# Sliding-window logits of the last 128 queries as two fp32r passes, and an order table with a third level

## The chip, the core and the metric

One core of a Trainium2 chip runs the kernel. The metric is device time in microseconds (us); the median of three runs is compared. Engines: PE is TensorE, DVE is VectorE, ACT is ScalarE, POOL is GpSimd, SP is SyncE, which issues the loads.

## The reference, cut to what matters

The model is a trunk of two layers over 256 tokens of width 1024 in fp32. The even layer has a gated linear attention (GLA, 4 heads) beside a sliding-window attention (SWA: 8 query heads on 2 key/value heads of width 64, window 128), then an output projection; the odd layer has 8 MoBA heads of width 128 and an output projection. The change touches the logits of SWA:

```python
qb = q.reshape(B_, NB, W, KVH, G, DH).transpose(0, 3, 4, 1, 2, 5)   # blocks of W = 128 queries
kb, vb = band(k), band(v)                                          # previous and own block: 256 keys
...
logits = jnp.einsum('bkgnqd,bknsd->bkgnqs', qb, kb).astype(jnp.float32) * (DH ** -0.5) + bias
logits = jnp.where(mask, logits, -jnp.inf)
...
probs = jax.nn.softmax(jnp.concatenate([logits, sink], axis=-1), axis=-1)[..., :-1]
o = jnp.einsum('bkgnqs,bknsd->bkgnqd', probs.astype(v.dtype), vb)
```

So the last 128 queries need, for each of 8 heads, a 128 x 256 product over 64 channels.

## The kernel before, in words

**Precision.** Most fp32 products are made of three fp32r products: an operand is split into a high part (its value rounded to fp32r) and a low part (the rest). `wh` and `wl` are the parts of a block of weights, `xh` and `xl` those of the activations, `pTh` and `pTl` those of the attention probabilities, `ogh` and `ogl` those of the gated outputs. A high part is a copy (`nc.copy`, on ACT or on DVE), a low part a subtraction (DVE). Projections write the PSUM tiles `pj`, logits the tiles `s`, transposes `t`, sums of attention `o`. The logits of SWA are plain fp32 matmuls in before, with `qT` and `kb` as they are; a tile `qT` has four heads in its 128 partitions, in two columns of blocks: for each pair of heads, key head 0 sits in partitions 0 to 63 and key head 1 in partitions 64 to 127.

**Order.** The code is recorded first, as nodes; `Plan.order` then simulates the engines and picks for each engine the ready node with the highest rank. A rank is the longest path of costs from the node to the end, plus a boost, plus numbers of the table `BOOST` for the node's stage (`nc.label`: "start", "bk", "bq", "swa1", ...) and for the stage with its engine ("swa1.PE"). `nc.together(pieces, cost)` joins several matmuls into one node; the first is then issued at line 179 and the others at line 160. Everything else is issued at line 179 too, so the names of tiles tell the work, save for a copy in its form for DVE, which has line 82. Tiles come from rings (4 `raw` buffers for loaded weights, 6 of `wh` and `wl`, 4 PSUM `pj`), and loads stand in the one queue of SP in order.

**SWA.** `swa(t)` makes the logits of query block t: for t = 0, 8 matmuls of 128 keys in one joined node; for t = 1, two joined nodes of 4 matmuls with 256 keys each, in the order head pair by head pair, with key heads 0 and 1 in turn, each on 64 rows of the array:

```python
for i, kv in nc.together([(i, kv) for i in its for kv in range(2)], 1450 if t else 1850):
    b = slice(64 * kv, 64 * kv + 64)
    nc.tensor.matmul(pvs[kv][:, i - i0, :], qb[i // 2][b, i % 2, t * P:(t + 1) * P], kb[b, 0:n],
                     start=True, stop=True)
```

Projections of other stages stand around these nodes on PE, as the table decides.

Of the kernel before, what the change touches and what calls it, by code (L numbers as in the profile page):

```python
# [11 lines left out]
F32 = mybir.dt.float32  # L12
F32R = mybir.dt.float32r
# [6 lines left out]
P = 128  # L20
D = 1024
S = 256
# [27 lines left out]
class Plan:  # L50
# [165 lines left out]
    def order(self):  # L216
        nodes = self.nodes
        for n in reversed(nodes):
            own = n.cost + n.tail + (2000 + n.dma / 400.0 if n.dma else 0)
            n.path = max((u.path + (n.cost + 2 if u.eng == n.eng == "PE" else own + self.latency(n, u))  # L220
                          for u in n.users if not u.load), default=own)
        for n in nodes:
            n.rank = 1e6 - n.idx if n.load else (
                n.path + n.boost + (BOOST.get(n.label, 0.0) + BOOST.get(n.label + "." + n.eng, 0.0)))
        clock = dict.fromkeys(self.ENGINES, 800.0)
        cand = {e: [] for e in self.ENGINES}
        table, dma = None, 0.0
        bank = {}

        def ready(n, e):  # L230
            return max([n.ready] + [t + self.latency(n, n) for b in n.banks for o, t in bank.get(b, {}).items() if o != e])

        for n in nodes:
            n.left, n.ready = len(n.deps), 0.0
            if not n.left:
                for e in n.forms:
                    cand[e].append(n)
        result, queue = [], [n.idx for n in nodes if n.eng == "SP"]
        while len(result) < len(nodes):
            best = None  # L240
            for e, c in cand.items():
                if e == "SP":
                    c = [n for n in c if n.idx == queue[0]] if queue else []
                if not c:
                    continue
                when = {n.idx: ready(n, e) for n in c}
                first = max(clock[e], min(when.values()))

                def gain(n):
                    return n.rank - (PENALTY if n.table and n.table != table else 0)  # L250

                pick = max((n for n in c if when[n.idx] <= first), key=gain)

                soon = [n for n in c if first < when[n.idx] <= first + LOOK and n.rank > gain(pick) + MARGIN]
                if soon and e != "SP":
                    pick = max(soon, key=lambda n: n.rank)
                    first = when[pick.idx]
                if best is None or (first, first + pick.forms[e][0]) < (best[0], best[0] + best[1].forms[best[2]][0]):
                    best = (first, pick, e)
            start, n, n.eng = best  # L260
            for e in n.forms:
                cand[e].remove(n)
            if n.eng == "SP":
                queue.pop(0)
            cost, tail, _ = n.forms[n.eng]
            if n.eng == "PE" and start < COLD:
                cost *= 1.85
            if n.table and n.table != table:
                table, cost = n.table, cost + 1283
            end = start + cost  # L270
            n.start = start
            clock[n.eng] = end
            if n.dma:
                dma = max(dma, start + (1500 if n.eng != "POOL" else 2500)) + n.dma / 400.0
                tail = dma + 500 + LATE - end
            result.append(n)
            for u in n.users:
                u.left -= 1
                u.ready = max(u.ready, end + 2 if u.eng == n.eng == "PE" else end + tail + self.latency(n, u))
                if not u.left:  # L280
                    for e in u.forms:
                        cand[e].append(u)
            n.end = end + tail
            for b in n.banks:
                bank.setdefault(b, {})[n.eng] = max(n.end, bank.get(b, {}).get(n.eng, 0.0))
        self.span = max(n.end for n in nodes)
        return result
# [6 lines left out]
SIZE = {F32: 4, F32R: 4, BF16: 2, I8: 1}  # L294


BOOST = {"start": 573258, "start.DVE": -38538, "start.POOL": 52750, "start.ACT": 1243, "start.PE": 40662, "rstd": 209951, "rstd.ACT": 127208, "rstd.DVE": 113369, "rstd.POOL": -103238, "rstd.PE": -63184, "bk": 369539, "bk.PE": 13356, "bk.DVE": 198, "bq": 14881, "bq.PE": -11180, "bq.DVE": -1220256, "decay": -52551, "decay.PE": 66981, "decay.ACT": 61712, "decay.DVE": 9116, "bg": 10969, "bg.ACT": -64523, "bg.PE": -41970, "swa0": -4537, "swa0.PE": -352320, "swa0.POOL": -37746, "swa0.DVE": -9500, "swa0.ACT": -51324, "aq": -112180, "aq.ACT": -85453, "aq.DVE": -223051, "aq.PE": 79963, "ak": -100825, "ak.ACT": 151115, "ak.PE": -242853, "swa1": 68756, "swa1.PE": 23420, "swa1.POOL": 181142, "swa1.DVE": -59955, "swa1.ACT": -94554, "gla": 18982, "gla.PE": 34789, "gla.ACT": -128852, "gla.DVE": -7061, "gla.POOL": 19304, "ag": -184974, "ag.ACT": -42703, "ag.DVE": -62205, "ag.PE": -215469, "agate": -1314, "agate.ACT": -116486, "agate.DVE": 11971, "agate.PE": 43490, "oe": -524223, "oe.ACT": -21502, "oe.DVE": -34920, "oe.PE": 17533, "h1": 4121, "h1.DVE": -77200, "h1.PE": -15335, "h1.ACT": 8186, "h1.POOL": 164832, "odd": -21419, "odd.PE": 30523, "odd.DVE": 68575, "cv": 3851, "cv.ACT": -41808, "cv.DVE": -1217, "cv.PE": 230720, "ck": -791503, "ck.ACT": 48816, "ck.DVE": 120, "ck.PE": 58567, "q0": 60721, "q0.ACT": -448094, "q0.DVE": 15032, "q0.PE": -52983, "g0": -464, "g0.ACT": 35308, "g0.DVE": 7665, "g0.PE": 13119, "moba0": -18143, "moba0.PE": 26122, "moba0.DVE": -25038, "moba0.ACT": 99267, "q1": 12325, "q1.ACT": -288835, "q1.DVE": -22989, "q1.PE": -4150, "g1": 4635, "g1.ACT": -23792, "g1.DVE": -131311, "g1.PE": 3161, "moba1": -8670, "moba1.PE": 15882, "moba1.DVE": 124820, "moba1.ACT": -179903, "oo": -68254, "oo.ACT": 638, "oo.DVE": -312970, "oo.PE": -5575, "tail": 23837, "tail.DVE": 29969, "tail.ACT": -40694, "tail.POOL": -8207, "tail.SP": -33334}
COLD = 6500
WARM = 7
PENALTY, LATE, LOOK, MARGIN = 12000, 600, 130, 1500  # L300
# [3 lines left out]
def trunk(ctx: ExitStack, tc: tile.TileContext, t_in, out):  # L304
    real, nc = tc.nc, Plan(tc.nc)
# [343 lines left out]
    def swa(t):  # L649
        n = P * (t + 1)  # L650
        probs = [[], []]
        for i0 in range(0, 4, 4 // (t + 1)):

            pts = [ps("s") for kv in range(2)]
            pvs = [pt.rearrange("p (h c) -> p h c", c=n) for pt in pts]
            its = range(i0, i0 + 4 // (t + 1))
            for i, kv in nc.together([(i, kv) for i in its for kv in range(2)], 1450 if t else 1850):
                b = slice(64 * kv, 64 * kv + 64)
                nc.tensor.matmul(pvs[kv][:, i - i0, :], qb[i // 2][b, i % 2, t * P:(t + 1) * P], kb[b, 0:n],
                                 start=True, stop=True)  # L660
            for kv in range(2):
                probs[kv] += softmax(t, [4 * kv + i for i in its], pvs[kv], 0, nsink)
        og = buf("og", [P, 4, P], F32, 2)
        low = buf("low", [P, 4, P])
        for kv in range(2):
            po = weigh(t, probs[kv], [(bvs[:, :, kv], 0), (bvs[:, :, kv], 1)])
            own, other = slice(64 * kv, 64 * kv + 64), slice(64 - 64 * kv, 128 - 64 * kv)
            nc.copy(low[own], po[other])
            nc.vector.tensor_add(og[own], po[own], low[own])
        gated(og, og, sgb, t, slice(0, P))  # L670
        to_operand(0, t, 4, og)
# [4 lines left out]
    kb = buf("kb", [P, S])  # L676
    nc.vector.tensor_mul(kb, o[:, 0], rr[0])


    nc.label = "bq"  # L680
    def bias_of(h, t, far):
# [5 lines left out]
                       ap=[list(a.ap[0]), [-first * step if t else P, n], [-1, P]])  # L687

    o = project_cols("bq", xh[0], xl[0], 1)
    qb = []  # L690
    for i in range(2):
        q = buf("qT", [P, 2, S], F32, 3)
        nc.vector.tensor_mul(q, o[i], rr[1].unsqueeze(1).to_broadcast([P, 2, S]))
        qb.append(q)

    nc.label = "decay"

# [69 lines left out]
    for t in range(NT):  # L767
        c0 = t * P
        pv = [ps("s")[:, 0:S].rearrange("p (h c) -> p h c", h=2) for e in range(2)]
        for j, e, half in nc.together([(j, e, i) for j in range(2) for e in range(2) for i in range(2)], 750):  # L770
            b = slice(64 * e, 64 * e + 64)
            if half == 0:
                nc.tensor.matmul(pv[e][0:64, j, :], ke[b, j, c0:c0 + 64], qx[b, j, c0:c0 + P], start=True, stop=True)
# [6 lines left out]


    pS = ps("o")
    for h in nc.together(range(4), 740):
        b = slice(64 * (h % 2), 64 * (h % 2) + 64)
        nc.tensor.matmul(pS[b, h * P:(h + 1) * P], kdt[:, h * 64:(h + 1) * 64], va[0][:, h * P:(h + 1) * P],
                         start=True, stop=True)
# [229 lines left out]
```

## Time and profile before

| | before |
|---|---|
| median of 3 runs | 213.86 us (213.02 to 214.02) |
| profiled execution, its own time | 213.65 us |
| its span in the trace | 211.9 us |
| granted TensorE clock, mean | 0.994 |
| PE busy | 202.8 us (96%), 1431 matmul records |
| PEld busy (weight loads) | 182.5 us (86%) |
| DVE busy | 175.6 us (83%) |
| ACT busy | 106.3 us (50%) |
| POOL busy | 13.5 us (6%) |
| chain that ended last | PE 82%, DVE 6%, DMA 5%, issue 4% |

Busy time is the union of the records of an engine. Matmuls are pipelined and a record lasts longer than the distance to the next one, so a gap of PE shows best in the distance from one start to the next. The last matmul starts at 205.28 us; what follows it up to 211.9 us is the tail. An fp32 matmul leaves two records, an fp32r matmul one.

### The profile page before, as it was taken

Reading aid. Unit: us, or ns where it says so; the run is one execution under the profiler, and the core shown is the slowest. Engines: PE = TensorE matmul, PEld = TensorE weight load, DVE = VectorE, ACT = ScalarE, POOL = GpSimd, SP = SyncE. Lnnn points to the kernel's source line nnn. Section 1 sums busy time; section 2 is a strip of 40 time slices with the busy share of each in tenths; the row PEclk is TensorE's granted clock in tenths of the full one; section 3 lists DMA queues with packets and bytes.
Section 4 is the critical chain, followed back from the end, with each engine's and each line's share of the span. In section 5 each row is a group of like instructions: output and inputs, shape, how many; then the busy total and the mean of one; then the engine's idle time right before and its main releaser. Section 6 shows DMA issues by size and latency. Waiting matters only on the chain.

```text
span 211.9 us, 3783 instructions
## 1 busy us (share of the span) xinstructions
PE 202.8 (96%) x1431; PEld 182.5 (86%) x1431; DVE 175.6 (83%) x365; ACT 106.3 (50%) x206; POOL 13.5 (6%) x38
## 2 busy tenths in 40 slices
PE   7899999999999999999999999999999999999970
PEld 2899999999977777887789999998999999788870
DVE  3997888998999999996985866996889998966551
ACT  3568544793789538462263700404386465910221
POOL 5007000000110000310001010000000000000101
PEclk9999999999999999999999999999999999999997
DMA  6998988786620003497045481087751443120012
GB/s 210 408 410 333 356 302 263 260 281 189 199 98 3 2 0 99 120 328 248 17 186 197 153 298 49 5 295 295 261 172 69 162 138 99 17 82 3 26 73 99
DMA packets 10913, 36.05 MB, mean 170 GB/s; under 512 B 1344, under 2 KB 1808, under 8 KB 10896
## 3 DMA queue, kind: packets, MB, share of 16 engines
q1 hardware_dynamic: 10464, 35.13, 47.7%
q10 hardware_dynamic: 432, 0.69, 0.9%
q8 instruction: 11, 0.18, 0.4%
q14 instruction: 6, 0.05, 0.1%
HBM read 34.76 MB, written 1.05 MB: 169 GB/s over the span
## 4 chain that ended last, share of the span: by engine, by line
PE 82%; DVE 6%; DMA 5%; issue 4%; SPq 1%; ACT 1%; POOLq 0%; POOL 0%; ACTq 0%; DVEq 0%
PE pj L179 63%; PE s L179 8%; PE o L179 7%; PE t L179 3%; DMA raw<-in_q 3%; DMA raw<-in_xav 2%; DVE neg L179 1%; PE s L160 1%; DVE wl L179 1%; DVE pTl L179 1%; DVE wh L82 1%; DVE pTh L82 1%; SPq L179 1%; ACT wh L179 1%; DVE junk L179 0%
## 5 line engine op out<-in xcount | busy, mean ns | idle before, releaser
L179 DVE TENSOR_TENSOR wl<-raw,wh 128x1024 fp32r<-128x1024 f32 (+2 forms) x59 | 68.1, 1169 | 6.5 <-ACT wh L179 3.4
L179 PE MATMUL pj<-xh,wh 128*128 128x256 f32 x224 | 56.1, 288 | 0.2 <-ACT wh L179 0.2
L179 PE MATMUL pj<-xh,wl 128*128 128x256 f32 x224 | 55.8, 287 | 0.0
L179 PE MATMUL pj<-xl,wh 128*128 128x256 f32 x224 | 55.5, 288 | 0.0
L179 ACT ACTIVATE wh<-raw 128x1024 fp32r<-128x1024 f32 (+2 forms) x37 | 37.4, 1017 | 32.9 <-DMA raw<-in_q 11.1
L179 PEld LDWEIGHTS pj<-xh,wh 128*128 128x128 f32 x224 | 39.2, 191 | 0.9 <-ACT wh L179 0.6
L179 PEld LDWEIGHTS pj<-xl,wh 128*128 128x128 f32 x224 | 39.3, 191 | 0.7 <-issue 0.3
L179 PEld LDWEIGHTS pj<-xh,wl 128*128 128x128 f32 x224 | 39.5, 191 | 0.4 <-DVE wl L179 0.2
L82 DVE CAST wh<-raw 128x1024 fp32r<-128x1024 f32 (+2 forms) x22 | 14.6, 666 | 12.4 <-PE pj L179 4.7
L179 PE MATMUL pj<-wl,ogh 128*128 128x512 f32 (+1 forms) x64 | 22.9, 373 | 0.0
L179 PE MATMUL pj<-wh,ogh 128*128 128x512 f32 (+1 forms) x64 | 22.6, 372 | 0.0
L179 PE MATMUL pj<-wh,ogl 128*128 128x512 f32 (+1 forms) x64 | 22.5, 371 | 0.0
L179 PE MATMUL pj<-wh,xl 128*128 128x328 f32 (+2 forms) x64 | 17.4, 336 | 0.6 <-DVE xl L179 0.6
L179 PE MATMUL pj<-wh,xh 128*128 128x328 f32 (+2 forms) x64 | 17.1, 332 | 0.2 <-DVE xh L82 0.2
L179 PE MATMUL pj<-wl,xh 128*128 128x328 f32 (+2 forms) x64 | 17.2, 332 | 0.0
L179 ACT ACTIVATE prob<-neg,mn 128x129 f32<-128x129 f32 (+3 forms) x32 | 14.2, 445 | 3.7 <-DVE mn L179 3.7
L179 PEld LDWEIGHTS pj<-wl,ogh 128*128 128x128 f32 x64 | 12.1, 189 | 2.2 <-DVE wl L179 0.6
L179 PEld LDWEIGHTS pj<-wh,ogl 128*128 128x128 f32 x64 | 12.0, 188 | 1.9 <-DVE ogl L179 0.3
L179 PEld LDWEIGHTS pj<-wh,xh 128*128 128x128 f32 x64 | 11.2, 188 | 2.5 <-DVE xh L82 1.1
L179 PEld LDWEIGHTS pj<-wh,ogh 128*128 128x128 f32 x64 | 11.9, 188 | 1.6 <-ACT ogh L179 0.2
L179 PEld LDWEIGHTS pj<-wh,xl 128*128 128x128 f32 x64 | 11.0, 188 | 1.5 <-DVE xl L179 1.1
L179 ACT ACT_TABLE_LOAD x8 | 10.3, 1283 | 3.8 <-DVE xt L179 1.3
(190 smaller groups left out, 332.5 us busy)
## 6 DMA issues: line engine op xcount, KB each, us to landing
raw<-in_oe SPq DMA_DIRECT2D x8, 512.0 KB, 4.0
raw<-in_q SPq DMA_DIRECT2D x8, 512.0 KB, 4.2
raw<-in_g SPq DMA_DIRECT2D x8, 512.0 KB, 4.4
raw<-in_oo SPq DMA_DIRECT2D x8, 512.0 KB, 3.4
raw<-in_bq SPq DMA_DIRECT2D x4, 512.0 KB, 6.5
raw<-in_bg SPq DMA_DIRECT2D x4, 512.0 KB, 6.0
raw<-in_ag SPq DMA_DIRECT2D x4, 512.0 KB, 4.9
raw<-in_xav SPq DMA_DIRECT2D x4, 456.0 KB, 5.2
```

The costliest lines, as they stand in the source:

```text
L82: lambda: getattr(self.vector._real, name)(*args, **kw))
L160: node.forms = {eng: (node.cost, node.tail, lambda: (emit(), getattr(real, method)(*args, **kw)))}
L179: node.forms = {eng: (node.cost, node.tail, lambda: getattr(real, method)(*args, **kw))}
```

## The change

First, the logits of `swa(1)` become fp32r. A new tile `kbs` has for each key head the high part of the keys twice (in both halves of the partitions) and the low part once (in its own half). A new tile `qs{i}{kv}` has the high part of the queries in its own half and the low part in the other half. Per head there are then two matmuls into the same PSUM region: one over all 128 rows (query high and low, stacked, on key high, twice), and one over 64 rows (query high on key low). They are not joined into one node. Making the tiles takes 8 copies and 6 subtractions of 64 x 256. Second, a rank may also take a number from the table for a stage, an engine and the name of the written tile. The table is new in whole (481 entries against 106). Third, the planner's cost of four joined nodes is lower.

```diff
             n.rank = 1e6 - n.idx if n.load else (
-                n.path + n.boost + (BOOST.get(n.label, 0.0) + BOOST.get(n.label + "." + n.eng, 0.0)))
+                n.path + n.boost + (BOOST.get(n.label, 0.0) + BOOST.get(n.label + "." + n.eng, 0.0)
+                                    + BOOST.get(n.label + "." + n.eng + "." + n.tag[1].split("_")[0], 0.0)))
...
-            for i, kv in nc.together([(i, kv) for i in its for kv in range(2)], 1450 if t else 1850):
-                b = slice(64 * kv, 64 * kv + 64)
-                nc.tensor.matmul(pvs[kv][:, i - i0, :], qb[i // 2][b, i % 2, t * P:(t + 1) * P], kb[b, 0:n],
-                                 start=True, stop=True)
+            if t:
+                for kv in range(2):
+                    b = slice(64 * kv, 64 * kv + 64)
+                    for i in its:
+                        q = qbs[kv, i // 2][:, i % 2]
+                        nc.tensor.matmul(pvs[kv][:, i - i0, :], q, kbs[:, kv, 0], start=True, stop=False)
+                        nc.tensor.matmul(pvs[kv][:, i - i0, :], q[b], kbs[b, kv, 1], start=False, stop=True)
+            else:
+                for i, kv in nc.together([(i, kv) for i in its for kv in range(2)], 1190):
+                    b = slice(64 * kv, 64 * kv + 64)
+                    nc.tensor.matmul(pvs[kv][:, i - i0, :], qb[i // 2][b, i % 2, 0:P], kb[b, 0:n], start=True, stop=True)
...
+    kbs = buf("kbs", [P, 2, 2, S], F32R)
+    for kv in range(2):
+        own, other = slice(64 * kv, 64 * kv + 64), slice(64 - 64 * kv, 128 - 64 * kv)
+        nc.copy(kbs[own, kv, 0], kb[own])
+        nc.copy(kbs[other, kv, 0], kb[own])
+        nc.vector.tensor_sub(kbs[own, kv, 1], kb[own], kbs[own, kv, 0].bitcast(F32))
...
+        for kv in range(2):
+            v = qbs[kv, i] = buf(f"qs{i}{kv}", [P, 2, P], F32R, 1, 512)
+            own, other = slice(64 * kv, 64 * kv + 64), slice(64 - 64 * kv, 128 - 64 * kv)
+            nc.copy(v[own], q[own, :, P:])
+            nc.vector.tensor_sub(v[other], q[own, :, P:], v[own].bitcast(F32))
...
-BOOST = {"start": 573258, "start.DVE": -38538, "start.POOL": 52750, ... }
+BOOST = {"start": 429806, "start.DVE": 47795, "start.DVE.warm0": -30025, ... }
```

In before, PE has the first joined node of the logits of the last 128 queries (`s` from `kb` and `qT`) in one block among the matmuls of a projection (`pj` from `xh`, `xl`, `wh`, `wl`); each row here is one fp32 matmul, and what follows is the first transposes of the probabilities (`t`):

```order
L179 MATMUL pj_73<-xh_71,wh_85 128x256
L179 MATMUL s_122<-kb_123,qT_125 128x256
L160 MATMUL s_124<-kb_123,qT_125 128x256
L160 MATMUL s_122<-kb_123,qT_125 128x256
L160 MATMUL s_124<-kb_123,qT_125 128x256
L179 MATMUL pj_73<-xl_72,wh_85 128x256
```

In the changed kernel the same place on PE has the four fp32r matmuls of key head 0 (128 rows, 64 rows, 128 rows, 64 rows, in this order), a stretch of the projection, and the four of key head 1:

```order
L179 MATMUL pj_73<-xh_71,wh_85 128x256
L179 MATMUL s_122<-kbs_124,qs_127 128x256 x4
L179 MATMUL pj_73<-xl_72,wh_85 128x256
...
L179 MATMUL pj_73<-xl_72,wh_85 128x256
L179 MATMUL s_125<-kbs_124,qs_128 128x256 x4
L179 MATMUL pj_73<-xh_71,wl_86 128x256
```

Further on, the second four heads: key head 0's second pair has one matmul on 128 rows, one on 64, then the four of key head 1 come between, and the last two (128 rows, then 64) stand on both sides of a product of probabilities and values (`o` from `pTh` and `bv`):

```order
L179 MATMUL pj_74<-wl_89,xh_71 128x512
L179 MATMUL s_122<-kbs_124,qs_130 128x256 x2
L179 MATMUL s_125<-kbs_124,qs_131 128x256 x4
L179 MATMUL s_122<-kbs_124,qs_130 128x256
L179 MATMUL o_70<-pTh_158,bv_116 128x512
L179 MATMUL s_122<-kbs_124,qs_130 128x256
L179 MATMUL pj_74<-wh_88,xh_71 128x512
```

What moved: 4 fp32 matmuls twice (16 records in all) became 16 fp32r matmuls, and the 64-row ones stand singly between 128-row ones.

At the program's start PE has in before the four `pj` tiles (`pj_73` and `pj_74` belong to the first 128 tokens, `pj_75` and `pj_76` to the last 128) in turn for each part of the first block of weights (`wh_79`, `wl_80`), and then the second block (`wh_82`):

```order
L179 MATMUL pj_73<-wh_79,xh_71 128x328
L179 MATMUL pj_75<-wh_79,xh_71 128x328
L179 MATMUL pj_74<-wh_79,xh_71 128x328
L179 MATMUL pj_76<-wh_79,xh_71 128x328
L179 MATMUL pj_73<-wh_79,xl_72 128x328
L179 MATMUL pj_75<-wh_79,xl_72 128x328
```

In the changed kernel:

```order
L179 MATMUL pj_73<-wh_79,xh_71 128x328
L179 MATMUL pj_75<-wh_79,xh_71 128x328
L179 MATMUL pj_74<-wh_79,xh_71 128x328
L179 MATMUL pj_73<-wh_79,xl_72 128x328
L179 MATMUL pj_74<-wh_79,xl_72 128x328
L179 MATMUL pj_73<-wl_80,xh_71 128x328
L179 MATMUL pj_74<-wl_80,xh_71 128x328
L179 MATMUL pj_74<-wh_82,xh_71 128x328
L179 MATMUL pj_73<-wh_82,xh_71 128x328
L179 MATMUL pj_74<-wh_82,xl_72 128x328
L179 MATMUL pj_73<-wh_82,xl_72 128x328
L179 MATMUL pj_76<-wh_79,xh_71 128x328
```

Two of the four tiles now run ahead into the second block of weights, and matmuls of the first block for the other two come later. DVE and ACT also share the splitting of the second block in another way: the copy `wh_82` moved from DVE to ACT, and its `xh` from ACT to DVE.

## Rows read from the trace of the kernel before

**Rows 1.** Windows: busy us and count of each engine, granted clock, DMA share, GB/s.

```profile
8.08:205.30 197.22, 196.49 (x1408) 179.15 (x1408) 169.33 (x350) 102.37 (x200) 9.82 (x22) 1.00 0.49 169
20.00:52.30 32.30, 32.30 (x271) 32.26 (x270) 28.96 (x49) 19.89 (x31) 0.86 (x2) 1.00 0.83 278
...
55.00:75.00 20.00, 19.55 (x116) 15.56 (x115) 19.52 (x68) 16.30 (x47) 1.48 (x8) 1.00 0.23 79
```

**Rows 2.** Timeline of PE at the start: start, duration, work, [idle before].

```profile
6.72 0.77 PE L179 MATMUL pj<-wh,xh 128*128 128x328 f32 x4
8.08 0.86 PE L179 MATMUL pj<-wh,xl 128*128 128x328 f32 x4 [0.59 <-DVE xl L179]
```

**Rows 3.** Timeline of PE, two waits: one in SWA, one in the odd layer.

```profile
67.43 0.41 PE L179 MATMUL t<-ident,prob 128*128 128x128 f32 x2 [0.15 <-DVE pTl L179]
...
146.63 0.51 PE L179 MATMUL pj<-xh,wh 128*128 128x256 f32 x2 [0.17 <-ACT wh L179]
```

**Rows 4.** Timeline of PE, the two logits nodes of the last 128 queries.

```profile
58.15 0.28 PE L179 MATMUL pj<-xh,wh 128*128 128x256 f32 x1
58.35 0.70 PE L179 MATMUL s<-kb,qT 64*128 64x256 f32 x2
...
59.91 0.39 PE L179 MATMUL pj<-xl,wh 128*128 128x256 f32 x1
60.13 0.28 PE L179 MATMUL pj<-xh,wl 128*128 128x256 f32 x1
...
62.00 0.40 PE L179 MATMUL pj<-wh,xl 128*128 128x512 f32 x1
62.33 0.48 PE L179 MATMUL s<-kb,qT 64*128 64x256 f32 x1
...
63.90 0.63 PE L179 MATMUL t<-ident,prob 128*128 128x128 f32 x4 [0.29 <-ACT prob L179]
```

**Rows 5.** Timeline of PE, the logits node of the first 128 queries.

```profile
52.42 0.28 PE L179 MATMUL pj<-xh,wl 128*128 128x256 f32 x1
52.55 0.28 PE L179 MATMUL pj<-xh,wh 128*128 128x256 f32 x1
52.76 0.37 PE L179 MATMUL s<-kb,qT 64*128 64x128 f32 x1
...
52.97 0.27 PE L179 MATMUL s<-kb,qT 64*128 64x128 f32 x1
52.98 0.94 PE L160 MATMUL s<-kb,qT 64*128 64x128 f32 x13
53.85 0.39 PE L179 MATMUL pj<-xl,wh 128*128 128x256 f32 x1
54.07 0.28 PE L179 MATMUL pj<-xh,wl 128*128 128x256 f32 x1
```

**Rows 6.** Timeline of PE, an fp32 matmul on 128 rows (odd layer).

```profile
149.06 0.28 PE L179 MATMUL pj<-xh,wl 128*128 128x256 f32 x1
149.18 0.38 PE L179 MATMUL s<-s,qT 128*128 128x128 f32 x2
...
149.52 0.28 PE L179 MATMUL pj<-xh,wl 128*128 128x256 f32 x1
```

**Rows 7.** Timeline of PE, logits in fp32r on 128 rows (odd layer).

```profile
171.87 0.28 PE L179 MATMUL s<-kbs,qs 128*128 128x256 f32 x1
171.99 0.40 PE L179 MATMUL o<-pTh,cv 128*128 128x512 f32 x1
```

**Rows 8.** Groups of instructions on DVE that write small tiles: count, duration ns min/median/max, starts.

```profile
L82 DVE CAST cv<-o x2: 404/408/413, 24.8 to 25.2; 16x256 fp32r<-16x256 f32 x2
...
L179 DVE TENSOR_TENSOR cv<-o,cv x1: 416/416/416, 28.4 to 28.4; 16x256 fp32r<-16x256 f32 x1
```

**Rows 9.** Timeline of DVE at the start.

```profile
7.54 0.88 DVE L179 SCALAR_TENSOR_TENSOR xl<-raw,xt,xh 128x256 fp32r<-128x256 f32 x2
```

**Rows 10.** Timeline of ACT at the start.

```profile
7.11 0.75 ACT L179 ACTIVATE wh<-raw 128x656 fp32r<-128x656 f32 x1 [0.55 <-DMA raw<-in_xav]
```

More of the change, by code (lines that the diff above doesn't have):

```diff
@@ L294 @@
 SIZE = {F32: 4, F32R: 4, BF16: 2, I8: 1}
-BOOST = {"start": 573258, "start.DVE": -38538, "start.POOL": 52750, "start.ACT": 1243, "start.PE": 40662, "rstd": 209951, "rstd.ACT": 127208, "rstd.DVE": 113369, "rstd.POOL": -103238, "rstd.PE": -63184, "bk": 369539, "bk.PE": 13356, "bk.DVE": 198, "bq": 14881, "bq.PE": -11180, "bq.DVE": -1220256, "decay": -52551, "decay.PE": 66981, "decay.ACT": 61712, "decay.DVE": 9116, "bg": 10969, "bg.ACT": -64523, "bg.PE": -41970, "swa0": -4537, "swa0.PE": -352320, "swa0.POOL": -37746, "swa0.DVE": -9500, "swa0.ACT": -51324, "aq": -112180, "aq.ACT": -85453, "aq.DVE": -223051, "aq.PE": 79963, "ak": -100825, "ak.ACT": 151115, "ak.PE": -242853, "swa1": 68756, "swa1.PE": 23420, "swa1.POOL": 181142, "swa1.DVE": -59955, "swa1.ACT": -94554, "gla": 18982, "gla.PE": 34789, "gla.ACT": -128852, "gla.DVE": -7061, "gla.POOL": 19304, "ag": -184974, "ag.ACT": -42703, "ag.DVE": -62205, "ag.PE": -215469, "agate": -1314, "agate.ACT": -116486, "agate.DVE": 11971, "agate.PE": 43490, "oe": -524223, "oe.ACT": -21502, "oe.DVE": -34920, "oe.PE": 17533, "h1": 4121, "h1.DVE": -77200, "h1.PE": -15335, "h1.ACT": 8186, "h1.POOL": 164832, "odd": -21419, "odd.PE": 30523, "odd.DVE": 68575, "cv": 3851, "cv.ACT": -41808, "cv.DVE": -1217, "cv.PE": 230720, "ck": -791503, "ck.ACT": 48816, "ck.DVE": 120, "ck.PE": 58567, "q0": 60721, "q0.ACT": -448094, "q0.DVE": 15032, "q0.PE": -52983, "g0": -464, "g0.ACT": 35308, "g0.DVE": 7665, "g0.PE": 13119, "moba0": -18143, "moba0.PE": 26122, "moba0.DVE": -25038, "moba0.ACT": 99267, "q1": 12325, "q1.ACT": -288835, "q1.DVE": -22989, "q1.PE": -4150, "g1": 4635, "g1.ACT": -23792, "g1.DVE": -131311, "g1.PE": 3161, "moba1": -8670, "moba1.PE": 15882, "moba1.DVE": 124820, "moba1.ACT": -179903, "oo": -68254, "oo.ACT": 638, "oo.DVE": -312970, "oo.PE": -5575, "tail": 23837, "tail.DVE": 29969, "tail.ACT": -40694, "tail.POOL": -8207, "tail.SP": -33334}
@@ L689, in trunk @@
     o = project_cols("bq", xh[0], xl[0], 1)
-    qb = []
+    qb, qbs = [], {}
     for i in range(2):
@@ L769, in trunk @@
         pv = [ps("s")[:, 0:S].rearrange("p (h c) -> p h c", h=2) for e in range(2)]
-        for j, e, half in nc.together([(j, e, i) for j in range(2) for e in range(2) for i in range(2)], 750):
+        for j, e, half in nc.together([(j, e, i) for j in range(2) for e in range(2) for i in range(2)], 700):
             b = slice(64 * e, 64 * e + 64)
@@ L782, in trunk @@
     pS = ps("o")
-    for h in nc.together(range(4), 740):
+    for h in nc.together(range(4), 595):
         b = slice(64 * (h % 2), 64 * (h % 2) + 64)
```

1 line of the change is left out of this document (added).

## The prediction

> **What bounds the kernel now.** I read the windows first, then the timeline of PE from start to start, then the waits. From 8.08 to 205.30 us PE is busy 196.49 of 197.22 us, at full granted clock [rows 1]: nothing but PE's own work, and the few places where it stands, can change the time by much. The reader should see in the same rows how close the others are. From 55 to 75, where the sliding-window attention runs, DVE is busy 19.52 of 20.00 us and ACT 16.30. From 20 to 52.3, where the new tiles must be made, DVE is busy 28.96 of 32.30 us, so it has 3.3 us of its own.
>
> Where does PE stand? At the start it waits 0.59 us before 8.08 for DVE's `xl` [rows 2]; from start to start that is 1.36 us for four matmuls that otherwise take 0.6 to 0.7. In SWA it stands before the transposes at 63.90 and 67.43, in the odd layer before 146.63 for ACT's `wh` [rows 3, 4]. The three are the sort of thing that another order can remove. How much each is worth I read from starts, since records overlap and the idle time shown is too small: 0.29 is shown at 63.90, while the starts lose 0.43 (below).
>
> **The logits, what goes.** The first joined node lies between the projection's matmuls at 58.15 and 60.13 [rows 4]. Two 256-column projection matmuls take 0.12 each, so the node holds PE for 1.98 − 0.24 = 1.74 us. The second starts after a 512-column matmul at 62.00 (0.23 long) and ends before 63.90: 1.67 us, of which some 0.43 is the wait on ACT's `prob`, and 1.24 the node. Together 2.98 us leave.
>
> **What comes.** 16 fp32r matmuls of 256 columns. On 128 rows one takes 0.12 from start to start: the odd layer's logits have this form, 171.87 to 171.99 [rows 7]. 16 × 0.12 = 1.92 us. If nothing else counted, this would gain 1.06 us.
>
> But eight of the 16 are on 64 rows, and each stands alone between matmuls on 128 rows, so that PE goes from one form to the other 16 times; before it was four times in the two nodes. What does one change of form cost? The node for the first 128 queries shows it cleanly, since nothing waits there [rows 5]. Projection matmuls come 0.12 apart (52.42, 52.55 with rounding). From the last of them to the first 64-row logits it is 0.21: 0.09 more. From there to the next pair it is again 0.21, where the later pairs need (52.98 + 0.94 − 0.27 − 52.98) / 6 = 0.11: 0.10 more, and the first record is longer too, 0.37 against 0.27. On the way back the same: the last pair starts at 53.65 and the first projection matmul at 53.85 (0.20 instead of 0.11), and the next at 54.07 (0.22 instead of 0.12), with a record of 0.39 against 0.28. So each change costs 0.09 before the first matmul of the new form and 0.10 behind it, about 0.195 us, in both directions; I read the second half as a weight load that could not be done ahead. Is it the fp32 form, and not the 64 rows? An fp32 matmul on 128 rows stands in the odd layer at 149.18: from 149.06 to 149.52 there are two projection matmuls and its two passes, 0.24 + 0.22 = 0.46, nothing left over [rows 6]. It is the rows.
>
> The Trainium skill says the same in "TensorEngine Tiling (Array Packing)", section Tiling Modes, Key Properties: a change of the tiling mode, other than of the tile, drains TensorE. By that sentence the change is charged at every alternation, which agrees with 0.21 against 0.12; it gives no figure for the weight load behind it.
>
> If all 16 pay in full: 1.92 + 16 × 0.195 = 5.04 us, against 2.98: **+2.06**. Bounds: with the 0.09 alone paid (the next weights loaded ahead after all), 1.92 + 16 × 0.095 = 3.44: +0.46; with no price at all, −1.06. I take the full price, because in [rows 5] both halves appear at both changes, and a 64-row matmul that stands alone has no second one in its form behind which a load could hide.
>
> **Making the tiles.** 8 copies and 6 subtractions of 64 x 256. Neither form is in the trace; DVE's time hangs on the columns, and 16 x 256 takes 0.41 for a copy and 0.416 for a subtraction [rows 8]. Ten of the 14 are DVE's in the changed order: 4.1 us, of which 2 us is paid back because two copies of weights and smaller ones go over to ACT in the same stretch. The other four are ACT's. All must be done by 58 us, and DVE has 3.3 us of idle time between 20 and 52.3 [rows 1], while PE there waits for nothing (32.30 of 32.30 busy), which leaves nothing to gain either. **0**, bounds 0 and +1.2: if 2 us of the 4.1 came in front of weights that PE is about to need, the cover would be gone.
>
> **The start.** Before, PE does four matmuls for each part, and stands up to 8.08 because DVE makes `xl` of the second block after `wh`, `wl` and `xh` of it; `xl` starts at 7.54 [rows 9]. After, ACT makes `wh` (0.75 us, [rows 10]) and DVE starts with `xh` and `xl`, so `xl` is there before 7. But two tiles run ahead: only seven matmuls of the first block stand in front of the first that needs `wh_82`, against twelve before. They are done around 6.1, and PE stands until some 6.85. The wait of 0.75 moves forward by a microsecond, it doesn't go; the five matmuls (5 × 0.15 = 0.75) left behind fill later waits for the next blocks of weights, of which the order before had none that long. Stepping through both orders by hand with the landing times of before, the 53rd matmul comes 0.5 us later. **+0.5**, bounds 0 (all of it filled in) and +0.8 (none).
>
> **Waits in SWA.** The order after gives `pTh` to ACT and puts the transposes of the second key head further back, behind projection work. The waits at 63.90 (0.43) and 67.43 (0.31) should go: **−0.74**, bounds 0 and −0.74. What is late next is DVE, which waits for the logits of key head 1, a matter of 1.3 us that PE's projection work hides.
>
> **Everything else in the table.** The same instructions in another order. In the odd layer PE's small waits sum to some 1.5 us, the one at 146.63 the largest [rows 3]; weights there come just in time, so a new order can remove some or make others. **0**, bounds −1.0 and +1.0.
>
> **Sum**, against the profiled execution's own 213.65 (span 211.9, 1.75 around it; the median is 0.21 higher): 213.65 + 2.06 + 0.5 − 0.74 = 215.47. I say **215.4**. A difference of 0.5%, 1.07 us, is about what a measurement of this kernel tells from none: under 212.8 counts as faster, over 214.9 as slower.
>
> **Rivals.**
>
> *The change of form costs half, or is hidden.* If the next weights do load ahead, the logits cost +0.46 and the whole 213.65 + 0.46 + 0.5 − 0.74 = 213.9: no change. For it: only the node of [rows 5] shows all four halves clean; the second node of [rows 4] shows the first of them (62.00 to 62.33, 0.33 against 0.23) and a wait covers its way back. Against: after the first node the 0.22 is there once more (59.91 to 60.13). Chance 0.25.
>
> *It is free: a gain.* The 64-row matmul adds to the same PSUM region with half of the same queries; were such an alternation free of the price that the joined nodes show, 16 × 0.12 would stand against 2.98, and the time would be 213.65 − 1.06 + 0.5 − 0.74 = 212.35, faster by 0.7%. The sign turns at a price of (2.98 − 1.92 + 0.24) / 16 = 0.08 per change (0.24 is what the start and the SWA waits leave), and a gain that can be told needs one under (1.30 − 1.07) / 16 = 0.015. Against it are both directions in [rows 5]. Chance 0.16, with the cases in which the table removes 1.5 us or more elsewhere besides a half price.
>
> *DVE uncovered.* DVE is at 98% from 55 to 75 [rows 1], and 55 to 75 is where the new logits land. If the later logits (key head 1 stands a whole projection stretch behind key head 0) push its chain of `neg`, `prob` and transposes back, the GLA and the gates behind come late, and PE runs out of projection work: +1.2 us more, 216.7. For it: DVE has only 0.5 us there. Against: PE still has ready matmuls of two stages at that point. Chance 0.12.
>
> *The forecast*, 214.6 to 216.3 by the bounds of the start and of the SWA waits: chance 0.47.
>
> **How the numbers follow.** Slower by over 0.5%: the forecast but for its lowest edge, and DVE uncovered, 0.55. Same: half price and the edge, 0.28. Faster 0.17. The range 212.6 to 216.8 leaves out most of the free case and the worst of the last. The likeliest case's own range is 214.6 to 216.3.
>
> **What would show it.** In the profile after: 64-row logits starting 0.3 us from their neighbours rather than 0.12, with records near 0.37; the 16 together about 5 us of PE. At the start a wait of PE near 6.1 to 6.85 and none near 8. No wait of PE before the transposes of SWA. The same tail behind the last matmul. I am wrong if the 64-row matmuls follow at 0.12, if PE waits for `kbs` or `qs`, or if the odd layer's waits change by more than a microsecond.

## The result, and the profile after

The changed kernel is slower: 215.95 us in the median of six runs (215.35 to 216.98) against 213.17 (212.88 to 214.02), a ratio of 1.0114 with a 95% interval of 1.0089 to 1.0139. The forecast was 215.4, slower, in a range of 212.6 to 216.8. In a second series of runs, beside other kernels, the ratio was 1.0103 (1.0077 to 1.0129).

The page of the changed kernel, its busy times and the chain that ended last by line:

```profile
span 214.9 us, 3791 instructions
...
PE 206.4 (96%) x1431; PEld 185.5 (86%) x1431; DVE 176.0 (82%) x362; ACT 115.6 (54%) x224; POOL 13.3 (6%) x38
...
PE pj L179 63%; PE s L179 9%; PE o L179 6%; PE t L179 3%; DMA raw<-in_q 3%; DMA raw<-in_xav 2%; ACT wh L179 2%; DVE wl L179 1%; DVE xt L179 1%; ACT prob L179 1%; DVE xr L179 1%; PE s L160 1%; ACT L179 1%; SPq L179 0%; DVE junk L179 0%
```

PE is as full as before: its records cover 3.6 us more, and the time without one is 0.6 us less (8.5 against 9.1). So PE's own work takes longer, for two reasons that show below: the logits, and a slow pace at the start of this execution. The windows show the same (busy us of PE, PEld, DVE, ACT, POOL; granted clock; DMA share; GB/s); they answer to [rows 1], moved by the 2 us that the logits of the first 128 queries came later:

```profile
20.00:54.30 34.30, 34.30 (x285) 34.27 (x284) 30.46 (x52) 25.06 (x39) 0.91 (x4) 1.00 0.75 255
55.00:75.00 20.00, 19.94 (x123) 15.96 (x122) 16.79 (x61) 16.29 (x47) 1.75 (x8) 1.00 0.23 84
```

PE has no idle time at all while the new tiles are made, and DVE is less busy from 55 to 75 than before, 16.79 us against 19.52 (with the work there moved back by the 2 us). The tiles cost DVE this (groups of instructions: count, duration ns min/median/max, starts):

```profile
L179 DVE TENSOR_TENSOR qs<-qT,qs x6: 419/422/684, 37.7 to 170.4; 64x256 fp32r<-64x256 f32 x4, 128x512 fp32r<-128x512 f32 x2
...
L82 DVE CAST kbs<-kb x2: 287/289/291, 27.6 to 27.9; 64x256 fp32r<-64x256 f32 x2
```

A subtraction is 0.42 us, as estimated from [rows 8]; a copy 0.29, not 0.41. All lie long before 60 us. The logits themselves, on PE's timeline (start, duration, work), answer to [rows 4]:

```profile
59.88 0.28 PE L179 MATMUL pj<-xh,wh 128*128 128x256 f32 x1
60.00 1.25 PE L179 MATMUL s<-kbs,qs 128*128 128x256 f32 x4
61.18 0.39 PE L179 MATMUL pj<-xl,wh 128*128 128x256 f32 x1
61.40 0.28 PE L179 MATMUL pj<-xh,wl 128*128 128x256 f32 x1
...
65.33 2.16 PE L179 MATMUL s<-kbs,qs 128*128 128x256 f32 x7
67.32 0.39 PE L179 MATMUL o<-pTh,bv 128*128 128x512 f32 x1
67.64 0.38 PE L179 MATMUL s<-kbs,qs 64*128 64x256 f32 x1
67.95 0.50 PE L179 MATMUL pj<-wh,xh 128*128 128x512 f32 x1
68.29 0.39 PE L179 MATMUL pj<-wh,xl 128*128 128x512 f32 x1
68.52 0.60 PE L179 MATMUL t<-ident,prob 128*128 128x128 f32 x4
```

A group counts its first form in its name, so the x4 holds two matmuls on 128 rows and two on 64. Four 256-column matmuls take 1.18 us from 60.00 to 61.18 and seven take 1.99 from 65.33 to 67.32, where 0.12 each would be 0.48 and 0.84. The single one at 67.64 follows a product of 512 columns by 0.32 instead of 0.23, is itself followed after 0.31, and the next after 0.34 instead of 0.23. From start to start the 16 matmuls lose 3.13 us against 0.12 each (their neighbours' second halves included). What the second half is, the rows of PEld (weight loads) show:

```profile
67.20 0.19 PEld L179 LDWEIGHTS o<-pTh,bv 128*128 128x128 f32 x1
67.64 0.18 PEld L179 LDWEIGHTS s<-kbs,qs 64*128 64x128 f32 x1 [0.25 <-issue]
67.95 0.19 PEld L179 LDWEIGHTS pj<-wh,xh 128*128 128x128 f32 x1
68.06 0.19 PEld L179 LDWEIGHTS pj<-wh,xl 128*128 128x128 f32 x1
```

Between two matmuls on 128 rows the next weights are loaded ahead: those of `o` from 67.20 for the matmul at 67.32, those of 68.06 for 68.29. At a change of rows the load starts only with its own matmul, at 67.64 and at 67.95.

The start answers to [rows 2]:

```profile
4.61 1.19 PE L179 MATMUL pj<-wh,xh 128*128 128x328 f32 x3 [0.18 <-DVE xh L82]
5.59 0.75 PE L179 MATMUL pj<-wh,xl 128*128 128x328 f32 x2
6.14 0.75 PE L179 MATMUL pj<-wl,xh 128*128 128x328 f32 x2
7.33 0.91 PE L179 MATMUL pj<-wh,xh 128*128 128x328 f32 x2 [0.44 <-ACT wh L179]
```

The wait moved forward, from before 8.08 to before 7.33, and its releaser from DVE's `xl` to ACT's `wh`. But two matmuls of 328 columns take 0.55 here (5.59 to 6.14), 0.273 each, where four take 0.6 to 0.7 in the stretch of [rows 2], 0.15 each. This pace holds up to 10.5 us, apart from the waits; the last section comes back to it. The logits of the first 128 queries start at 54.73 instead of 52.76 us.

In SWA the waits for the transposes became shorter without going (they answer to [rows 3, 4]): the transposes at 72.61 start 0.45 behind a matmul of 0.23, 0.22 lost, those of 76.95 lose 0.15 in the same way; before it was 0.43 and 0.31.

```profile
72.17 0.39 PE L179 MATMUL pj<-wh,xh 128*128 128x512 f32 x1
72.61 0.63 PE L179 MATMUL t<-ident,prob 128*128 128x128 f32 x4
```

### The profile page after: what moved, and what is told of

Its sections match the earlier page's. It is cut to its first block, busy times and chain, and to the rows that moved or that the text cites. A ratio compares the mean times of both kernels' runs of the same rounds, so it can differ in the third digit from the quotient of the medians.

```text
span 214.9 us, 3791 instructions
## 1 busy us (share of the span) xinstructions
PE 206.4 (96%) x1431; PEld 185.5 (86%) x1431; DVE 176.0 (82%) x362; ACT 115.6 (54%) x224; POOL 13.3 (6%) x38
## 4 chain that ended last, share of the span: by engine, by line
PE 82%; DMA 5%; issue 4%; ACT 3%; DVE 3%; SPq 0%; POOLq 0%; POOL 0%; ACTq 0%; DVEq 0%
PE pj L179 63%; PE s L179 9%; PE o L179 6%; PE t L179 3%; DMA raw<-in_q 3%; DMA raw<-in_xav 2%; ACT wh L179 2%; DVE wl L179 1%; DVE xt L179 1%; ACT prob L179 1%; DVE xr L179 1%; PE s L160 1%; ACT L179 1%; SPq L179 0%; DVE junk L179 0%
## 5 line engine op out<-in xcount | busy, mean ns | idle before, releaser
L179 PE MATMUL pj<-xh,wl 128*128 128x256 f32 x224 | 60.0, 287 | 0.0
L179 PE MATMUL pj<-xh,wh 128*128 128x256 f32 x224 | 59.7, 286 | 0.2 <-DVE xt L179 0.2
L179 PE MATMUL pj<-xl,wh 128*128 128x256 f32 x224 | 59.7, 286 | 0.0
L179 ACT ACTIVATE wh<-raw 128x1024 fp32r<-128x1024 f32 (+2 forms) x39 | 39.3, 1019 | 31.8 <-PE pj L179 12.1
L179 PEld LDWEIGHTS pj<-xh,wh 128*128 128x128 f32 x224 | 40.9, 191 | 0.7 <-issue 0.4
L179 PEld LDWEIGHTS pj<-xl,wh 128*128 128x128 f32 x224 | 41.0, 191 | 0.2
L179 PE MATMUL pj<-wh,xh 128*128 128x328 f32 (+2 forms) x64 | 20.6, 358 | 0.6 <-ACT wh L179 0.4
L179 PE MATMUL pj<-wh,xl 128*128 128x328 f32 (+2 forms) x64 | 19.9, 345 | 0.0
L179 PE MATMUL pj<-wl,xh 128*128 128x328 f32 (+2 forms) x64 | 19.6, 338 | 0.0
L179 PEld LDWEIGHTS pj<-wl,xh 128*128 128x128 f32 x64 | 12.4, 200 | 0.6
```

The costliest lines, as they stand in the source:

```text
L179: node.forms = {eng: (node.cost, node.tail, lambda: getattr(real, method)(*args, **kw))}
```

## The experiments

My theory after this: the logits lose 2.05 us, nearly all of it by 16 changes between 64 and 128 rows; the new order at the start costs about half a microsecond; the rest of the table about nothing. Rivals: the price lies in something else than the rows; the start costs all of 2 us; the table as a whole is what counts. All times are medians of the runs of a series, and ratios are to the kernel before in the same series of runs (213.63 us for `e1` to `e4`, 213.94 for `e5` to `e8`; each run's label stands in brackets).

**The changed kernel again.** (`e1`) No edit.

> The changed kernel itself, unaltered, for a second profile and for times on the same chip as the next three. In its first profile the matmuls of 328 columns between 4.61 and 10.5 us came 0.273 us apart, in that of before 0.15. Theory A (the slow stretch belongs to the changed order at the start): it is there again, to about 10.5 us, and the logits of the first 128 queries start near 54.7 us, 2.0 later than before. Theory B (the moment of the clock's rise falls by chance, and the first profile caught a late one): the matmuls come 0.15 apart from about 4.9 us, the logits of the first 128 queries start near 53.3, and this profiled execution takes about 1 us less than the first (216.98). Ratio to before 1.007 to 1.013.

216.02 us, ratio 1.0103 (1.0077 to 1.0129). PE's timeline at the start:

```profile
4.61 1.11 PE L179 MATMUL pj<-wh,xh 128*128 128x328 f32 x3 [0.19 <-DVE xh L82]
5.55 0.46 PE L179 MATMUL pj<-wh,xl 128*128 128x328 f32 x2
...
7.73 0.57 PE L179 MATMUL pj<-wh,xh 128*128 128x328 f32 x2 [1.41 <-ACT wh L179]
```

and ACT's, which made that `wh`:

```profile
6.93 0.75 ACT L179 ACTIVATE wh<-raw 128x656 fp32r<-128x656 f32 x1 [2.16 <-DMA raw<-in_xav]
```

The slow pace ends at about 5.5 us this time, so it doesn't belong to the order. Yet the logits of the first 128 queries start at 54.17: 1.4 us behind before, where Theory B had put 53.3. What took its place is a later landing: the second block of weights came at 6.93 instead of 6.53. The profiled execution took 216.28 us, 0.7 less than the first and not the 1 expected. The first stretch varies by itself, with either order (see the start as before, below).

**All 128 rows in the second pass.** (`e2`)

```diff
-                        nc.tensor.matmul(pvs[kv][:, i - i0, :], q[b], kbs[b, kv, 1], start=False, stop=True)
+                        nc.tensor.matmul(pvs[kv][:, i - i0, :], q, kbs[:, kv, 1], start=False, stop=True)
...
         nc.vector.tensor_sub(kbs[own, kv, 1], kb[own], kbs[own, kv, 0].bitcast(F32))
+        nc.gpsimd.memset(kbs[other, kv, 1].bitcast(F32), 0.0)
```

> The second pass of the logits (query high on key low) runs over all 128 rows, the low keys padded with zeros in the other half by POOL; instructions and their order on PE stay as in the changed kernel. Theory A (the price is the change of form between 64 and 128 rows, 16 times 0.195 = 3.1 us): the 16 matmuls start 0.12 apart, 1.9 us of PE in all, and the time falls by about 3.1 us against the changed kernel in the same call, to 0.5 us below to 1 us above before. Theory B (the price lies in the accumulation into one region of PSUM, or in the odd weights of fp32r): starts stay 0.3 apart and the time doesn't move by more than 0.5 us.

212.57 us, ratio 0.9952 (0.9933 to 0.9971): 3.45 us below the changed kernel of the same series, and 1.06 us below before, where at most 0.5 below was expected. PE's timeline at the first four heads:

```profile
58.26 0.28 PE L179 MATMUL pj<-xh,wh 128*128 128x256 f32 x1
58.37 0.68 PE L179 MATMUL s<-kbs,qs 128*128 128x256 f32 x4
58.89 0.28 PE L179 MATMUL pj<-xl,wh 128*128 128x256 f32 x1
59.01 0.28 PE L179 MATMUL pj<-xh,wl 128*128 128x256 f32 x1
...
64.27 0.60 PE L179 MATMUL t<-ident,prob 128*128 128x128 f32 x4
```

Four matmuls in 0.52 us instead of 1.18, into the same PSUM regions, with the same types, in the same places. Half of each second pass multiplies by zero, and it is the cheaper one. The price is that of the change of rows.

How much of the 3.45 is it? The traces have the same order on PE in both kernels, so they can be set side by side. From the first of the 16 matmuls to the transposes behind the last it is 8.52 us in both profiles of the changed kernel (60.00 to 68.52 above) and 5.90 here (58.37 to 64.27): 2.62 us. That is less than 3.13, since the 16 take 2.31 us and not 1.92: at 60.09, 62.34 and 62.75 PE now has to wait for DVE. Of the 3.71 us between this profile and the repeated one of the changed kernel (212.57 and 216.28), 1.07 lie before the first logits, where the kernels do not differ on PE: the start of that execution was a faster one.

**Half of it.** (`e6`) Only key head 0 gets 128 rows (`r = b if kv else slice(0, P)` in place of `b`, and the zeros for key head 0 alone).

> Only key head 0 gets its second pass on all 128 rows; key head 1 keeps the 64-row one. 8 changes of form are left of 16. Theory A (a fixed price for each change): half of the gain of all 128-row passes, 1.5 to 1.7 us below the changed kernel, and the 64-row matmuls that are left still start 0.31 from their neighbours. Theory B (the price comes with the first change of a block, or with a stretch as a whole): either nothing or nearly all of the 3.2 us.

214.78 us, ratio 1.0041 (1.0019 to 1.0063). PE's timeline at both key heads of the first four heads:

```profile
58.34 0.67 PE L179 MATMUL s<-kbs,qs 128*128 128x256 f32 x4
58.85 0.28 PE L179 MATMUL pj<-xl,wh 128*128 128x256 f32 x1
...
60.04 1.32 PE L179 MATMUL s<-kbs,qs 128*128 128x256 f32 x4
61.29 0.39 PE L179 MATMUL pj<-xh,wl 128*128 128x256 f32 x1
...
65.58 0.60 PE L179 MATMUL t<-ident,prob 128*128 128x128 f32 x4
```

Key head 0 takes 0.51, key head 1 still 1.25. In ratios 16, 8 and 0 changes stand at 1.0103, 1.0041 and 0.9952, steps of 1.3 us (1.5 to 1.7 were expected) and 1.9. The traces, which leave the start out, have equal steps: from the first of the 16 to the transposes behind the last 8.52, 7.24 and 5.90 us, 1.28 for the first eight changes and 1.34 for the other eight. So the price is a fixed one for each change, 0.16 to 0.17 us in the time and 0.195 where no wait takes part of it back.

**The start as before.** (`e3`) The entries of the stage "start" in the table are those of before; on PE only the first hundred rows or so differ from the changed kernel (the lines are shortened, and the new ones put in the order of the table of before).

```diff
-BOOST = {"start": 429806, "start.DVE": 47795, "start.DVE.warm0": -30025, ... "start.POOL.am10": 118119, ...
+BOOST = {"start": 573258, "start.DVE": -38538, "start.POOL": 52750, "start.ACT": 1243, "start.PE": 40662, ...
```

> The table's entries for the stage start are those of before, all others those of the changed kernel. On PE only the first 110 rows or so change. Theory A (the two tiles that run ahead at the start cost, as predicted, 0.5 us): 0.3 to 0.8 us less than the changed kernel. Theory B (they cost about 2 us, since PE stands once more and the clock comes up late): 1.5 to 2.2 us less, and the matmuls of the first stretch come 0.15 apart. Theory C (start is worth nothing, all of the loss lies in the logits): within 0.3 us of the changed kernel.

215.49 us, ratio 1.0082 (1.0059 to 1.0105): 0.5 below the changed kernel, with intervals that overlap. Theory B is out; between A and C this does not decide. In this execution the slow pace lasts to 7.3 us with the order of before:

```profile
4.40 1.46 PE L179 MATMUL pj<-wh,xh 128*128 128x328 f32 x4
5.66 1.29 PE L179 MATMUL pj<-wh,xl 128*128 128x328 f32 x4
6.75 1.01 PE L179 MATMUL pj<-wl,xh 128*128 128x328 f32 x4
```

**Both together** (`e5`), the start's entries of before and all 128 rows.

> Both single edits of the first call together: second pass on all 128 rows, and the table's entries of the stage start as before. If the two terms are separate (Theory A), they add: 3.2 to 3.5 us for the first, 0.5 for the second, so about 3.8 us below the changed kernel, some 212.1 us or 0.993 of before. Theory B (the start gains nothing once PE has 3 us less to do later, because the landing of weights takes over): no more than the first edit alone, 0.995 of before.

212.90 us, ratio 0.9956 (0.9936 to 0.9977): no better than 128 rows alone, as Theory B had it. The two pairs (1.0103 to 1.0082, 0.9952 to 0.9956) put what the order of the start costs at 0.5 us and at 0, each with 0.6 to 0.7 us either way. The second pair is not the start alone: in this profile PE waits 0.4 us before 24.3 for ACT's `ad` and 0.3 us near 107 for DVE's `xt`, which it does not in the profile with the start as before.

**The old table with the new logits.** (`e4`) The table of before, and its planner costs of the four joined nodes.

> The new logits (16 fp32r matmuls, tiles kbs and qs) with the table and the planner costs of before. Theory A (sum of the prediction by parts: logits +2.06, the rest of the loss is the new table's): 2 us above before, ratio 1.008 to 1.012, if the scheduler finds as good a place for the new copies. Theory B (the new table was needed to hide the copies and subtractions of the new tiles): 3 us and more above before, with waits of PE between 20 and 60 us. Theory C (the logits are not the loss): within 0.7 us of before.

228.82 us, ratio 1.0703 (1.0678 to 1.0727), 15 us above before. PE's timeline shows where the later logits have gone, and what they wait for:

```profile
84.33 1.32 PE L179 MATMUL s<-kbs,qs 128*128 128x256 f32 x4
87.20 1.32 PE L179 MATMUL s<-kbs,qs 128*128 128x256 f32 x4 [1.54 <-DVE qs L179]
...
89.68 0.47 PE L160 MATMUL s<-xt 64*64 64x128 f32 x1 [0.81 <-DVE mn L179]
```

Theory B has the size. The last heads' logits run at 84 to 88 us instead of 62 to 63 in before, and the last subtraction for `qs` comes at 86.7, 43 us after the changed kernel's (43.7). Most of the waits lie behind 60 us, not between 20 and 60, where PE is idle for 2.3 us.

**The old table with 128 rows.** (`e7`)

> Table and planner costs of before, new logits, second pass on all 128 rows. With the 64-row pass this was 15 us above before. Theory A (there the loss is in waits: the old table places the new tiles and the logits so that PE stands): still 10 us or more above before, 3 us less than with the 64-row pass. Theory B (the changes of form do it there too): within 3 us of before.

226.30 us, ratio 1.0570 (1.0535 to 1.0605). The changes of rows are worth 2.5 us to 3 us here too. Of the other 12 a good half are waits of PE, which is idle for 16.6 us of the span against 9.1 in before. The longest, in the waits of PE (us in total, times, longest):

```profile
PE s L179 <- DVE qs L179: 1.8, 1, 1.8
PE s L179 <- DVE mn L179: 1.4, 1, 1.4
PE o L179 <- DVE cv L179: 1.3, 1, 1.3
```

From 60.00 to 85.05 us PE is idle for 3.3 of 25.05, and behind that the granted clock falls to 0.50, the lower of its two levels (1.2 GHz instead of 2.4), for 10.24 us:

```profile
85.05:95.29 10.24, 8.77 (x50) 5.39 (x50) 6.04 (x18) 3.93 (x12) 0.37 (x2) 0.50 0.00 1
```

PE is busy for 8.77 us of it, so up to 4.4 us go to the clock (an estimate: half of 8.77). In `e4` there are three such stretches between 62.19 and 103.15 us, with PE busy for 12.7 us in all.

**The new table with the old logits** (`e8`) (the fp32 matmuls joined in fours with the cost 1450; no `kbs`, no `qs` in the even layer).

```diff
-            if t:
...
+            for i, kv in nc.together([(i, kv) for i in its for kv in range(2)], 1450 if t else 1190):
...
-    kbs = buf("kbs", [P, 2, 2, S], F32R)
...
```

> The new table and costs with the fp32 logits of before (joined in fours, planner cost 1450), without the new tiles. Theory A (the table is fitted to its own set of instructions, and crossing it costs in either direction): several us above before, with waits of PE in the stretch from 50 to 100 us. Theory B (the new table is the better one by itself and only the logits cost): 0.5 to 1 us from before, that is 2 us below the changed kernel.

220.25 us, ratio 1.0291 (1.0249 to 1.0333), 6 us above before. PE waits in the odd layer this time, for weights:

```profile
137.93 0.28 PE L179 MATMUL pj<-xh,wl 128*128 128x256 f32 x1
140.48 0.38 PE L179 MATMUL pj<-xh,wl 128*128 128x256 f32 x1 [2.27 <-DVE wl L179]
```

The waits were expected between 50 and 100 us. In SWA they lose about 1 us against 0.74 in before; most of the rest is here. From 137.00 to 146.49 us PE is busy for 5.72 of 9.49 us, and behind that the granted clock is at 0.50 for 3.4 us. Crossing costs in both directions; what a table is worth can't be read from exchanging it.

## Why the prediction was right

**The logits** were the main term and were right in mechanism and size: +2.06 forecast; in the profile 16 × 0.12 + 3.13 = 5.05 us in place of 2.98, so +2.07. That the price is in the rows is shown by the kernel with 128 rows in all passes, and that it comes with each change by the one with half of them. The size, 3.12 by the sum, is 3.13 by the starts; taking the changes away gives back 2.62 in the traces, because waits for DVE come to light. That the medians differ by 3.45 (3.2 by ratios), close to the 3.12, owes something to the starts of these executions. The second half of the price, a weight load that is not done ahead, is seen in the rows of PEld. The rival "half price" is refuted by starts 0.31 apart, the rival "free" by the same.

**The tiles** cost nothing, as said: PE is busy 34.30 of 34.30 us while they are made. DVE's ten take 3.7 us, not 4.1: a copy takes 0.29, the `cv` that stood for it 0.41. That this hangs on the table was not in the prediction: with the old one the last of the same tiles come some 40 us later and PE waits for them. The bound of +1.2 is for the order of the changed kernel and says nothing of another.

**DVE uncovered** did not come; DVE has 3.2 us free from 55 to 75.

**The SWA waits** were over-sized: 0.37 of the 0.74 is left, so the term is about −0.4.

**The start** was forecast at +0.5 by stepping through by hand with one execution's landing times. The exchange of the start's entries gives 0.5 once and 0 once, as far as medians can tell. The traces show how little one execution says: up to the first logits the two profiles of the changed kernel lose 2.1 and 1.5 us against before, those of the two kernels with the same start and 128 rows (`e2`, `e6`) 0.5 and 0.4, and the one with the start as before (`e3`) 0.8. (Before has one projection matmul more ahead of that point; its 0.12 is counted in.) In the profile shown above some 1.4 of the 2.1 are the slow pace: the matmul at 7.33, behind the wait, loses 0.18 and the ten after it 0.12 each. The five slow ones ahead of the wait cost nothing, since PE has to wait for `wh` anyway.

**Everything else in the table** was put at 0 with bounds of 1 us either way, and the traces give it a size. From the first logits to the last matmul it is 152.53 us in before, and 153.63, 153.49 and 153.47 in the three profiles that have the changed order there (the changed kernel twice, `e3`): 0.8 to 1.0 us more, with the projection matmul of 0.12 counted in. The logits make +2.07 of that and the SWA waits −0.4, so the rest of the table gained 0.7 to 0.9 us. The wait of the odd layer before 146.63 [rows 3], for example, has no counterpart.

**Around the span.** The forecast took 1.75 us between a run's time and its span for both kernels. In every run of before whose span is on record it is 1.66 to 1.79, in every run of the changed kernel 2.05 to 2.11: +0.35 that the sum does not have. The new table with the old logits has 1.69 to 1.72, the old table with the new ones 1.77 to 1.84. What makes it was not tried.

**The sum.** Forecast +1.8 us; measured +2.8 in the first series (interval 1.90 to 2.96) and +2.4 in the second (1.65 to 2.75). The mechanism and the main term were right, but that the rest came so close is in part luck. The 0.35 around the span was missing in it, the start cost more than 0.5 us in both profiles, and the waits were over-sized; the gain in the rest of the table took much of this back. The time itself, 215.95 for a forecast of 215.4, looks closer than the change, because before came out at 213.17 in that series, 0.5 below the 213.65 from which the forecast counts. How the start's own part divides into order, pace and landings stays open.

The version with 128 rows in all passes beats both kernels, by 0.5% and 1.5%. Its −1.06 us by medians equals the gain of the logits that the prediction gave for a price of nothing (1.92 against 2.98), but by chance: in its trace the logits gain 0.67 (2.31 against 2.98), the SWA waits and the rest of the table some 1.1, and the start and the time around the span lose 0.5 and 0.35.

## What to carry to other kernels

Price a matmul by what stands beside it: a 64-row matmul alone between 128-row ones cost 0.39 us beside its own 0.12 here, and padding it with zeros to 128 rows took the 0.39 away (2.62 us net for eight of them, after new waits). Keep small forms together in one block, as the joined nodes of before did, or don't use them. Set traces of the same order beside each other stretch by stretch before the medians are split into causes. And a table of priorities belongs to the instruction list that it was made for: compare a change of the work with the order held fixed (the 128-row edit left PE's order as it was), not by swapping tables.

## What the runs showed of the hardware beyond that

The pace of the first matmuls differs between executions of one kernel. In all ten profiles the warm-up matmuls of 512 columns come 0.427 us apart up to 3.79 us (0.40 for the first gap), which is 1.2 columns per ns, the pace of the lower of the two clock levels (1.2 GHz); the first projection matmul follows at 4.40 to 4.86. The 328-column matmuls go at 0.273 us (again 1.2 columns per ns) until 10.5 us in the first profile of the changed kernel, 5.5 in the second and 7.3 in the one with the start as before; in before they come 0.15 apart from 4.87 on. PE's work before 4.4 is the same. The column of the granted clock shows 1.00 in all these stretches, but it takes the time ahead of the trace's first clock record for full. Those records begin, at the full level, at 10.54, 5.49, 7.27 and 4.61 us, where the pace rises: the pace is the clock. In such a stretch it has to be read from starts:

```profile
4.60:10.50 5.90, 5.45 (x18) 5.01 (x19) 5.07 (x11) 3.11 (x7) 0.00 (x0) 1.00 0.98 371
```

This row is the window of the changed kernel's first profile in which 18 matmuls of 328 columns took 5.9 us; in the trace of before 32 start in the same window. Together with the landing of the second block of weights (ACT starts on it between 5.36 us in the profile with half of the rows padded and 6.93 in the repeated one) it moves the end of the first projection between 20.5 and 22.2 us in one and the same order, and may be what spreads the times of one kernel over 1.5 us here; that was not tried.
